# A two-layer encoder trunk on one core: order of work at the borders between its stages

## The chip, the core and the metric

The kernel runs on one core of a Trainium2 chip. A core has a matrix engine (TensorE, PE in the profile; its weight loads are shown apart as PEld), a vector engine (VectorE, DVE), an activation engine (ScalarE, ACT), a general engine (GpSimd, POOL) and a queue that issues nearly all transfers (SyncE, SP). Each engine runs its own list of instructions in order; where an instruction needs a result of another engine it waits, and all that stands behind it on its engine waits with it. The metric is the device time of one execution in microseconds (us); less is better.

## The reference

One token stream of 1024 rows and 1024 columns passes through a layer A and a layer B, all in fp32:

```python
h = rmsnorm(x, a_norm1); z = h @ a_w_in                  # layer A
tok   = gmlp_spatial_gating(gelu(z[u]), gelu(z[v]), ...)
mem_o = memory_attention(z[q], mem, ...)
x = x + concat(tok, mem_o) @ a_w_out
x = x + conv_ffn(rmsnorm(x, a_norm2), ...)
k, v, log_f_cum = split(rmsnorm(x, kv_norm) @ w_kv)      # shared by layer B
tok   = forgetting_attention(q, k, v, log_f_cum)         # layer B
x = x + concat(tok, mem_o) @ b_w_out
x = x + conv_ffn(rmsnorm(x, b_norm2), ...)
return rmsnorm(x, final_norm)

def conv_ffn(x, w_in, conv_w, conv_b, w_out):            # 1024 -> 2 x 2816 -> 1024
    h = x @ w_in
    hc = conv_b + sum(conv_w[j] * shifted(h, 2 - j) for j in range(3))
    gate, up = hc[:, :2816], hc[:, 2816:]
    return (silu(gate) * up) @ w_out
```

## The kernel before

Each fp32 matrix operand is split into a high part (a cast, on ACT) and a low part (value minus high part, on DVE or POOL), and each product is three matmuls: high by high, high by low, low by high. The feed-forward products are done block-wise with seven products in place of eight.

The stages, once for each layer:

- **Output projection** (`mix_out`, L575). For each of eight columns, in the order of the list `NORD` (0, 4, 1, 5, 2, 6, 3, 7), `mix_part` (L561) runs 48 matmuls (in layer B the first two columns have most of theirs behind them), and DVE adds the two halves from PSUM to the residual `xT[n]` (L573, the read-out). Then ACT scales (L583), the column is stored to `xdram`, its square goes into a sum `S` (L342 on POOL), and, every second column, `x_ops` (L598) forms the differences (`td`, L601) and splits (L346 on ACT, L347 on DVE) that the first stage of the feed-forward needs. The column's weights are a stream: raw tile `wr`, high part `wh` (L217, ACT), low part `wl` (L218, POOL).
- **Pairs** (`ffn`, function `pair`). 22 pairs of hidden blocks, seven products each. `w_prep` (L646 to L667) is a generator in seven steps that turns a pair's raw weights into seven split tiles `wo`: a cast on ACT (L646), a subtraction (L648; five of the seven on POOL, two on DVE), and four sums `ws` on DVE (L654, L655, L660, L667). In pair i it makes the weights of pair i+1; the weights of the first pair are made ahead of the pairs, by `drain(first[2])`, written ahead of `mix_out`. A pair's convolution (`conv`, L704 to L713) runs as another generator inside the next pair; that of the last pair was drained before the next stage is written.
- **Out phase** (`out_phase`). Seven products, each over six units (five of two blocks, one of one block): first `p1`, then `p5` and `p6` by turns, then `p3`, `p7`, `p2`, `p4`. The operands of a unit are loaded (`ro`, L793), some are combined on DVE (L813), and `both` splits them: a cast on ACT (L805) and a subtraction (L806) on DVE, or on POOL for one of the two operands where `both` is called with True. `ahead` keeps this two units ahead of PE. During `p1` the residual comes back from `xdram` in eight loads of 512 KB (L896); in layer B PE transposes it (L143, `to_rows`). `take` (L891) adds the finished PSUM banks to the residual. The last product, `p4`, ends column by column: its last two units run for one column, `take` reads it out, `on_done` handles it, then comes the next column. In layer B `on_done` is the final norm (L1640 on ACT, L1642, L1643 and L1647 on DVE, `rpow` L301 on POOL between them) and the store.
- At the end of layer A's out phase `before_last` is called after unit 2 of `p2` and after units 0 and 1 of `p4`: it loads the memory tokens, takes their norm, transposes them (`mem_t`: four steps of four PE transposes and a split of the result), and converts the first weight of the K/V projection.

A scheduler sets the order on each engine from the order in which the code is written, from readiness and from priorities; a `take` is fastened with `keep_in_program_order`. In layer A the residual arrives as high and low parts `xh`, `xl` and is put together again by `merge_residual`: eight additions of 128x1024 on POOL (L361), written before `mix_out`.

## Time and profile before

| | |
|---|---|
| median of 3 runs | 2295.09 us (2292.44 to 2295.14) |
| the profiled execution | 2295.76 us, of which the span in the trace is 2294.0 us |
| PE busy | 2150.1 us, 94% |
| DVE busy | 1724.6 us, 75% |
| ACT busy | 1035.8 us, 45% |
| POOL busy | 839.1 us, 37% |
| mean granted clock of PE | 0.982 of full speed |

The rows below come from the profile's page and from three kinds of answers of its trace. A row of the timeline gives the start and the length in us, the engine, the line, the operation, the tile written and the tiles read, the shape and how many such instructions follow each other; in brackets stands how long the engine was idle before it and what ended that wait. A row of the windows gives, for a stretch of the span, each engine's busy time with its count of instructions, then the granted clock of PE (1.00 is 2.4 GHz, 0.50 is 1.2 GHz), the share of time in which the DMA engines were busy, and GB/s.

### The profile page before, as it was taken

The numbers are of one execution on the slowest core, as the hardware profiler recorded it, in microseconds if no ns is written. First come the engines' busy times: TensorE is split into PE (matmuls) and PEld (weight loads), VectorE is DVE, ScalarE is ACT, GpSimd is POOL, SyncE is SP. The second block draws the span as 40 slices with busy tenths as digits, with TensorE's granted clock in tenths as the row PEclk, the third lists the DMA queues.
The fourth block names the chain that finished last, engine by engine and source line by source line (L and its number), as shares of the span: only waits on it lengthen the run. The fifth ranks groups of instructions, "written<-read, shape, count | busy, mean of one in ns | idle before, by whom it ended". The sixth has DMA issues, their size and how long they took to land.

```text
span 2294.0 us, 29435 instructions
## 1 busy us (share of the span) xinstructions
PE 2150.1 (94%) x10657; PEld 1791.2 (78%) x10657; DVE 1724.6 (75%) x2528; ACT 1035.8 (45%) x1732; POOL 839.1 (37%) x618
## 2 busy tenths in 40 slices
PE   7999799999999999989899999779999999999997
PEld 6998687777777878878688787667777777777886
DVE  4745748888888899566776777784888888886965
ACT  6562334343344434344555555653543344444433
POOL 1320633333333300351545554554333333331033
PEclk9999899999999999999999999999999999999999
DMA  5311221222222585513332333323222222256463
GB/s 177 93 29 37 65 97 61 83 83 83 77 80 83 192 279 178 180 33 85 109 78 80 91 98 98 86 73 101 67 83 83 75 82 83 68 201 236 147 202 111
DMA packets 219166, 243.55 MB, mean 106 GB/s; under 512 B 10074, under 2 KB 155648, under 8 KB 219020
## 3 DMA queue, kind: packets, MB, share of 16 engines
q1 hardware_dynamic: 218880, 241.63, 33.2%
q8 instruction: 84, 1.38, 0.3%
q14 instruction: 62, 0.51, 0.1%
q10 hardware_dynamic: 140, 0.04, 0.0%
HBM read 192.29 MB, written 38.85 MB: 101 GB/s over the span
## 4 chain that ended last, share of the span: by engine, by line
PE 30%; DVE 10%; issue 4%; ACT 3%; DMA 3%; POOL 2%; DVEq 0%; POOLq 0%; ACTq 0%; SPq 0%
PE pa L137 27%; PE pc L137 2%; DVE X L708 2%; DVE X L706 2%; PE pc L143 2%; DVE P L1368 1%; DMA nb<-cdram 1%; ACT P L1374 1%; POOL wo L648 1%; DVE X L347 1%; DVE ws L667 1%; DVE X L438 1%; DVE PTl L347 1%; DMA X<-xdram 1%; DVE U L727 1%
## 5 line engine op out<-in xcount | busy, mean ns | idle before, releaser
L137 PE MATMUL pa<-X,wo 128*128 128x512 f32 x3696 | 856.1, 392 | 25.5 <-DVE U L727 20.7
L137 PEld LDWEIGHTS pa<-X,wo 128*128 128x128 f32 x3696 | 690.9, 188 | 188.3 <-DVE U L727 37.7
L137 PE MATMUL pa<-X,X 128*128 128x512 f32 (+2 forms) x1868 | 445.3, 382 | 19.4 <-DVE sm L1368 8.5
L137 PEld LDWEIGHTS pa<-X,X 128*128 128x128 f32 x1868 | 343.9, 191 | 90.7 <-DVE sm L1368 8.7
L137 PE MATMUL pa<-X,wh 128*128 128x512 f32 (+1 forms) x1216 | 356.7, 403 | 17.8 <-ACT wh L217 8.6
L648 POOL TENSOR_TENSOR wo<-raw,wo 128x512 fp32r<-128x512 f32 x132 | 226.8, 1719 | 317.9 <-ACT wo L646 314.3
L137 PEld LDWEIGHTS pa<-X,wh 128*128 128x128 f32 x1216 | 220.9, 191 | 64.2 <-DVE X L347 11.2
L646 ACT CAST wo<-ws 128x512 fp32r<-128x512 f32 x176 | 109.1, 621 | 305.0 <-PE pa L137 293.1
L805 ACT CAST X<-ro 128x1024 fp32r<-128x1024 f32 (+1 forms) x142 | 130.5, 965 | 176.1 <-DVE ro L813 66.7
L137 PE MATMUL pa<-X,wl 128*128 128x512 f32 (+1 forms) x608 | 196.3, 402 | 12.4 <-POOL wl L218 12.3
L806 POOL TENSOR_TENSOR X<-ro,X 128x1024 fp32r<-128x1024 f32 (+1 forms) x34 | 89.1, 2630 | 320.2 <-ACT X L805 309.1
L648 POOL TENSOR_TENSOR wo<-ws,wo 128x512 fp32r<-128x512 f32 x88 | 116.4, 1323 | 219.6 <-ACT wo L646 212.9
L218 POOL TENSOR_TENSOR wl<-wr,wh 128x1024 fp32r<-128x1024 f32 (+1 forms) x41 | 102.2, 2494 | 213.4 <-ACT wh L217 208.1
L806 DVE TENSOR_TENSOR X<-ro,X 128x1024 fp32r<-128x1024 f32 (+1 forms) x108 | 137.0, 1294 | 49.8 <-ACT X L805 45.9
L137 PE MATMUL pa<-wh,X 128*128 128x256 f32 (+1 forms) x800 | 167.8, 288 | 0.0
L137 PEld LDWEIGHTS pa<-X,wl 128*128 128x128 f32 x608 | 111.2, 191 | 33.5 <-POOL wl L218 13.5
L137 PEld LDWEIGHTS pa<-wh,X 128*128 128x128 f32 x800 | 132.7, 190 | 1.6
L646 ACT CAST wo<-raw 128x512 fp32r<-128x512 f32 x132 | 81.1, 614 | 94.7 <-PE pa L137 89.9
L347 DVE TENSOR_TENSOR PTl<-pc,PTh 128x512 fp32r<-128x512 f32 (+1 forms) x152 | 90.8, 602 | 35.8 <-ACT PTh L346 34.6
L137 PE MATMUL pa<-wl,X 128*128 128x256 f32 (+1 forms) x400 | 113.8, 284 | 2.2 <-POOL wl L218 2.2
L467 POOL TENSOR_SCALAR P<-P,sm 128x128 f32<-128x128 f32 (+3 forms) x96 | 76.9, 802 | 90.2 <-DVE sm L1375 83.1
L1374 ACT ACTIVATE P<-P,sm 128x128 f32<-128x128 f32 (+3 forms) x96 | 74.7, 778 | 74.4 <-DVE sm L1368 72.4
(196 smaller groups left out, 3359.6 us busy)
## 6 DMA issues: line engine op xcount, KB each, us to landing
ro<-hdram SPq DMA_DIRECT2D x67, 512.0 KB
raw<-in_a_ffn_in_dram SPq DMA_DIRECT2D x44, 512.0 KB
hdram<-X SPq DMA_DIRECT2D x44, 512.0 KB
raw<-in_b_ffn_in_dram SPq DMA_DIRECT2D x44, 512.0 KB
ro<-in_a_ffn_out_dram SPq DMA_DIRECT2D x35, 512.0 KB
ro<-in_b_ffn_out_dram SPq DMA_DIRECT2D x32, 512.0 KB
X<-X SPq DMA_DIRECT2D x80, 128.0 KB
xdram<-X SPq DMA_DIRECT2D x16, 512.0 KB
```

The lines of the kernel that those rows point to most:

```text
L137: ins = nc.tensor.matmul(*a, **k)
L143: ins = nc.tensor.transpose(*a)
L218: eng.tensor_tensor(lo, raw, f32(hi), ALU.subtract)
L347: nc.vector.tensor_tensor(lo, src, f32(hi), ALU.subtract)
L467: nc.gpsimd.tensor_scalar(p, p, rinv, 1.0, ALU.mult, ALU.mult)
L646: nc.scalar.copy(h, src)
L648: eng.tensor_tensor(l, src, f32(h), ALU.subtract)
L706: nc.vector.scalar_tensor_tensor(t[:, 1:], h[:, :S - 1], w1, t[:, 1:], ALU.mult, ALU.add)
L708: nc.vector.scalar_tensor_tensor(t[:, 2:], h[:, :S - 2], w0, t[:, 2:], ALU.mult, ALU.add)
L805: nc.scalar.copy(h, src)
L806: (nc.gpsimd if pool else nc.vector).tensor_tensor(l, src, f32(h), ALU.subtract)
L1374: nc.scalar.activation(p[:, :n], p[:, :n], AF.Exp, bias=mn, scale=-1.0, accum_out=rs)
```

## The change

Five things are written in another place or for another engine:

1. `merge_residual` is gone. Layer A first converts the weights of the first two columns, then merges the residual in the order `NORD`, alternately on POOL and DVE (four each). The first pair's `w_prep` is no longer drained ahead of `mix_out`: `mix_out` calls `before(at)` ahead of each column, which takes one step (in layer A from the second column on, in layer B from the first); what is left is drained behind `mix_out`.
2. The convolution of the last pair is passed to `out_phase`, which takes two of its steps after each unit of `p1` and drains it before `take(a, 0, 0)`.
3. In `p1`, `both` is called without True, so that the six subtractions that stood on POOL in each layer go to DVE.
4. `before_last` is called after all four of the first units of `p4`; the memory transposes take one step at the second, third and fourth of these calls, and the fourth step behind the out phase.
5. The last read-outs, `take(a, 1, 0, [j])`, are not fastened to the program order.

```diff
-    def merge_residual(xh, xl):
-        res = []
-        for h, l in zip(xh, xl):
-            t = xt_()
-            nc.gpsimd.tensor_tensor(t, f32(l), f32(h), ALU.add)
...
-    def mix_out(tp, wget, kof, mh, ml, xT, g):
+    def mix_out(tp, wget, kof, mh, ml, xT, g, before):
...
         for at, n in enumerate(NORD):
+            before(at)
             xn = xT[n]
...
-                return both(a11s[u], lb(0, 0, u), True)
+                return both(a11s[u], lb(0, 0, u))
...
-        def take(bank, r, c, js=range(4)):
+        def take(bank, r, c, js=range(4), pin=True):
             for j in js:
                 d = acc[j + 4 * r][:, c * CH:(c + 1) * CH]
-                tc.keep_in_program_order(nc.vector.tensor_tensor(d, bank[j], d, ALU.add))
+                ins = nc.vector.tensor_tensor(d, bank[j], d, ALU.add)
+                if pin:
+                    tc.keep_in_program_order(ins)
...
-        def out_phase():
+        def out_phase(cg):
...
+                for _ in range(2):
+                    next(cg, None)
+            drain(cg)
             drain(rows)
             take(a, 0, 0)
...
             for u in range(NU - TAILU):
                 run(a, "p4", u, False)
-                if u < 2 and before_last is not None:
-                    before_last(u + 1)
+                before_last(u + 1)
...
-                take(a, 1, 0, [j])
+                take(a, 1, 0, [j], False)
                 on_done(j + 4, acc[j + 4])
...
-        drain(cg)
-        out_phase()
+        out_phase(cg)
...
-    xT = merge_residual(xh, xl)
...
     first = ffn_first(tp, a_ffn_in[0])
+    xT = {}
+
+    ast.conv(ast.at["o", NORD[0]] + 2)
+    for i, n in enumerate(NORD):
+        xT[n] = xt_()
+        (nc.vector if i % 2 else nc.gpsimd).tensor_tensor(xT[n], f32(xl[n]), f32(xh[n]), ALU.add)
+
+    def before_a(at):
+        if at > 0:
+            next(first[2], None)
+
+    ops, ssum_a = mix_out(
+        tp, lambda n: ast.use(("o", n), 1)[0], lambda at: KORD, mixh, mixl, xT, g_a2, before_a)
     drain(first[2])
-    ops, ssum_a = mix_out(tp, lambda n: ast.use(("o", n), 1)[0], lambda at: KORD, mixh, mixl, xT, g_a2)
...
         elif stage == 1:
             rm.append(mem_norm(tp, mtok, "T", 4))
             rm.append([])
-            drain(mem_t(mtok, rm[1]))
+            mt_g.append(mem_t(mtok, rm[1]))
         else:
-            wk_first[0] = wconv(wk_first[0], g_kv, True)
+            next(mt_g[0])
+            if stage == 2:
+                wk_first[0] = wconv(wk_first[0], g_kv, True)
...
     first = ffn_first(tp, b_ffn_in[0])
-    drain(first[2])
     ops, ssum = mix_out(
         tp, lambda n: wst.use(("o", n), 1)[0], lambda at: [6, 7] if at < NPRE else range(KT),
-        mixh, mixl, xT, g_b2)
+        mixh, mixl, xT, g_b2, lambda at: next(first[2], None))
+    drain(first[2])
```

How this moves instructions is shown at three places, before first, then after. Line numbers of the code behind the change are a few lower there (L648 reads L641, L793 reads L786, L217 and L218 stay).

POOL at the start of layer A's `mix_out`. `X` are the merged residual, `wo` the split weights of the first pair, `wl` the low parts of a column's weights, `S` the sum of squares. Before, these rows follow on six other merges and on the `wl` of the second column; the last row is the third column's:

```order
L361 TENSOR_TENSOR X_2418<-X_112,X_104 128x1024
L361 TENSOR_TENSOR X_2420<-X_113,X_105 128x1024
L648 TENSOR_TENSOR wo_2432<-raw_2426,wo_2432 128x512
L648 TENSOR_TENSOR wo_2440<-raw_2426,wo_2440 128x512
L648 TENSOR_TENSOR wo_2449<-ws_2430,wo_2449 128x512
L648 TENSOR_TENSOR wo_2452<-raw_2428,wo_2452 128x512
L648 TENSOR_TENSOR wo_2456<-ws_2444,wo_2456 128x512
L218 TENSOR_TENSOR wl_2616<-wr_2464,wh_2615 128x1024
```

Behind the change, from the `wl` of the second column on:

```order
L218 TENSOR_TENSOR wl_2419<-wr_2332,wh_2418 128x1024
L1206 TENSOR_TENSOR X_2422<-X_106,X_98 128x1024
L1206 TENSOR_TENSOR X_2426<-X_107,X_99 128x1024
L641 TENSOR_TENSOR wo_2502<-raw_2410,wo_2502 128x512
L1206 TENSOR_TENSOR X_2430<-X_108,X_100 128x1024
L1206 TENSOR_TENSOR X_2434<-X_109,X_101 128x1024
L218 TENSOR_TENSOR wl_2597<-wr_2439,wh_2596 128x1024
L218 TENSOR_TENSOR wl_2670<-wr_2505,wh_2669 128x1024
L342 TENSOR_TENSOR S_2438<-S_2438,sq_2562 128x1024
```

Between the second column's `wl` and the third's stand four merges and one subtraction instead of eight and five. On ACT one cast of the first pair, instead of seven, stands ahead of the third column's `wh`; on DVE four merges stand ahead of the first read-out, in place of four sums and two subtractions.

ACT in layer B's `mix_out`, between the third column and the fourth. `wo` are casts of the first pair's weights, `X<-td` and `X<-X` the casts of the differences of columns 0 and 4, `wh_14285` (before) and `wh_14275` (after) the fourth column's weights:

```order
L646 CAST wo_14127<-raw_14113 128x512
L646 CAST wo_14133<-ws_14130 128x512
L646 CAST wo_14136<-ws_14117 128x512
L646 CAST wo_14139<-raw_14115 128x512
L646 CAST wo_14143<-ws_14131 128x512
L346 CAST X_14196<-td_14194 128x512
L346 CAST X_14199<-X_14186 128x512
L346 CAST X_14204<-td_14202 128x512
L346 CAST X_14207<-td_14192 128x512
L346 CAST X_14212<-td_14210 128x512
L346 CAST X_14215<-X_14186 128x512
L217 CAST wh_14285<-wr_13977 128x1024
```

```order
L639 CAST wo_14199<-raw_14113 128x512
L346 CAST X_14177<-td_14175 128x512
L346 CAST X_14180<-X_14167 128x512
L346 CAST X_14185<-td_14183 128x512
L346 CAST X_14188<-td_14173 128x512
L217 CAST wh_14275<-wr_13977 128x1024
L346 CAST X_14193<-td_14191 128x512
L346 CAST X_14196<-X_14167 128x512
```

Four casts of the first pair and two of the differences moved behind the fourth column's `wh`. On DVE two sums (L660, L667) and one subtraction (L648) that stood ahead of these differences moved behind them, and on POOL two subtractions moved behind the fourth column's `wl`.

SP at the start of layer B's out phase, before and after. `X<-xdram` are the loads of the residual, `hdram<-X` the store of a pair's result, `ro` the operands:

```order
L793 DMA ro_18158<-in_b_ffn_out_dram 128x2x512
L793 DMA ro_18160<-in_b_ffn_out_dram 128x2x512
L793 DMA ro_18234<-in_b_ffn_out_dram 128x2x512
L793 DMA ro_18310<-in_b_ffn_out_dram 128x2x512
L793 DMA ro_18390<-in_b_ffn_out_dram 128x2x512
L896 DMA X_17950<-xdram 128x1024
L713 DMA hdram<-X_17904 128x1024
L896 DMA X_17952<-xdram 128x1024
```

```order
L786 DMA ro_18158<-in_b_ffn_out_dram 128x2x512
L891 DMA X_17939<-xdram 128x1024
L891 DMA X_17941<-xdram 128x1024
L891 DMA X_17943<-xdram 128x1024
L891 DMA X_17945<-xdram 128x1024
L891 DMA X_17947<-xdram 128x1024
L891 DMA X_17949<-xdram 128x1024
L891 DMA X_17951<-xdram 128x1024
L891 DMA X_17953<-xdram 128x1024
L786 DMA ro_18160<-in_b_ffn_out_dram 128x2x512
L786 DMA ro_18226<-hdram 128x2x512
L786 DMA ro_18234<-in_b_ffn_out_dram 128x2x512
```

The eight loads of the residual moved ahead of four loads of `p5`'s operands, and the store of the last pair's result moved behind them. POOL has nothing to do in `p1` any more, and PE's first transposes of the residual stand after the second unit of `p1`, where before they stood inside the third.

On DVE at the very end, where before each of the last four read-outs stood behind the whole final norm of the column before, the third read-out now stands right behind the second, and the fourth between the two small sums of the third column's norm.

## Rows read from the trace of the kernel before

**Rows 1.** The page: busy time of each engine, share of the span, instructions.
```profile
PE 2150.1 (94%) x10657; PEld 1791.2 (78%) x10657; DVE 1724.6 (75%) x2528; ACT 1035.8 (45%) x1732; POOL 839.1 (37%) x618
```

**Rows 2.** Timeline of PE at the start of layer A's output projection.
```profile
238.38 1.17 PE L137 MATMUL pa<-X,wh 128*128 128x512 f32 x4
...
261.43 1.20 PE L137 MATMUL pa<-X,wh 128*128 128x512 f32 x4 [0.58 <-ACT wh L217]
274.61 1.22 PE L137 MATMUL pa<-X,wl 128*128 128x512 f32 x2 [11.98 <-POOL wl L218]
275.63 1.91 PE L137 MATMUL pa<-X,wh 128*128 128x512 f32 x4
```

**Rows 3.** Timeline of the same stretch: POOL, then ACT, then DVE.
```profile
237.58 2.40 POOL L218 TENSOR_TENSOR wl<-wr,wh 128x1024 fp32r<-128x1024 f32 x1 [23.72 <-ACT wh L217]
243.53 21.24 POOL L361 TENSOR_TENSOR X<-X,X 128x1024 f32<-128x1024 f32 x8 [3.55 <-DVE X L347]
...
270.54 1.71 POOL L648 TENSOR_TENSOR wo<-ws,wo 128x512 fp32r<-128x512 f32 x1
272.21 5.14 POOL L218 TENSOR_TENSOR wl<-wr,wh 128x1024 fp32r<-128x1024 f32 x2
...
260.34 1.04 ACT L217 CAST wh<-wr 128x1024 fp32r<-128x1024 f32 x1
...
256.88 2.90 DVE L667 TENSOR_TENSOR ws<-raw,ws 128x512 f32<-128x512 f32 x1
```

**Rows 4.** Timeline at the start of layer A's out phase: PE, POOL, DVE.
```profile
808.06 8.23 PE L137 MATMUL pa<-X,X 128*128 128x512 f32 x35 [2.97 <-DVE X L806]
...
798.92 8.00 POOL L806 TENSOR_TENSOR X<-ro,X 128x1024 fp32r<-128x1024 f32 x3 [3.25 <-ACT X L805]
...
802.37 3.43 DVE L813 TENSOR_TENSOR ro<-ro,ro 128x1024 f32<-128x1024 f32 x1
```

**Rows 5.** Timeline of PE at the end of layer A's out phase.
```profile
983.29 0.66 PE L143 MATMUL pc<-ident,mt 128*128 128x128 f32 x4 [2.12 <-DVE X L347]
...
994.33 7.21 PE L137 MATMUL pa<-X,X 128*128 128x512 f32 x30 [0.84 <-DVE X L806]
1002.69 6.87 PE L137 MATMUL pa<-X,X 128*128 128x512 f32 x29 [1.15 <-DVE X L806]
```

**Rows 6.** Timeline in layer B's output projection: PE, DVE, POOL.
```profile
1549.70 2.50 PE L137 MATMUL pa<-X,wh 128*128 128x512 f32 x5 [7.54 <-ACT wh L217]
1552.56 1.22 PE L137 MATMUL pa<-X,wl 128*128 128x512 f32 x2 [0.36 <-POOL wl L218]
...
1534.57 0.68 DVE L655 TENSOR_TENSOR ws<-ws,raw 128x512 f32<-128x512 f32 x1
...
1534.67 2.86 POOL L342 TENSOR_TENSOR S<-S,sq 128x1024 f32<-128x1024 f32 x1 [1.17 <-ACT sq L338]
```

**Rows 7.** Timeline at the start of layer B's out phase: PE, POOL, SP.
```profile
2067.78 4.21 PE L137 MATMUL pa<-X,X 128*128 128x512 f32 x9 [4.05 <-POOL X L806]
...
2078.99 0.33 PE L143 MATMUL pc<-ident,X 128*128 128x128 f32 x1 [0.96 <-DMA X<-xdram]
...
2061.97 8.08 POOL L806 TENSOR_TENSOR X<-ro,X 128x1024 fp32r<-128x1024 f32 x2 [14.36 <-ACT X L805]
...
2053.29 8.13 SPq L793 DMA_DIRECT2D ro<-in_b_ffn_out_dram  x5
```

**Rows 8.** Windows of the same stretch, by 5 us.
```profile
2070.00:2075.00 5.00, 5.00 (x17) 3.85 (x16) 0.00 (x0) 0.00 (x0) 0.05 (x1) 0.70 1.03 415
```

**Rows 9.** Timeline of DVE at the end of layer B.
```profile
2275.09 0.69 DVE L891 TENSOR_TENSOR X<-pa,X 128x512 f32<-128x512 f32 x1 [8.87 <-PE pa L137]
...
2286.90 0.68 DVE L891 TENSOR_TENSOR X<-pa,X 128x512 f32<-128x512 f32 x1
2288.43 0.16 DVE L1642 TENSOR_TENSOR sm<-sm 128x1 f32<-128x1 f32 x1 [0.85 <-ACT jk L1640]
...
2289.50 1.41 DVE L1647 SCALAR_TENSOR_TENSOR X<-X,sm,X 128x512 f32<-128x512 f32 x2 [0.72 <-POOL sm L301]
```

More of the change, by code (lines that the diff above doesn't have):

```diff
@@ L679, in ffn_first, with ffn @@
         return in_srcs, w, w_prep(tp, raws, w, True)
-    def ffn(ops, ssum, first, w_out, cvs, on_done, tp, tm, before_last=None):
+    def ffn(ops, ssum, first, w_out, cvs, on_done, tp, tm, before_last=lambda stage: None):
         in_srcs, w, _ = first
@@ L951, in out_phase @@
                 run(c, "p2", u, True)
-                if u == 2 and before_last is not None:
+                if u == 2:
                     before_last(0)
@@ L1232 @@
     GSEQ = [2, 0, 1]
-    wk_first = []
+    wk_first, mt_g = [], []
     def before_last(stage):
```

3 lines of the change are left out of this document (1 added, 2 removed).

## The prediction, made before the changed kernel was run

> **What bounds the kernel now.** I read the page first: PE is busy for 94% of the span and no other engine for more than 75% [rows 1]. The arithmetic of PE is the same before and after, so the change can only win idle time of PE and time in which its clock is low. That is why I went through PE's timeline for idle stretches, and then for each through the timelines of the engine named in its bracket, to see what stood ahead of the awaited instruction. The stretches that the change touches are few. The largest is the third column of layer A's output projection: PE waits 0.58 us for the column's high part and then 11.98 us for its low part [rows 2]; the low part is the 272.21 row of POOL, which stands behind 21.24 us of merges and five subtractions [rows 3]. Next come layer B's projection (7.54 and 0.36 us, [rows 6]), the start of its out phase (4.05 us for POOL and three waits for loads of the residual, the last 0.96 us, some 2.2 us together [rows 7]), layer A's out phase at its start (2.97 us, [rows 4]) and its end (2.12, 0.84 and 1.15 us, [rows 5]). The end of the kernel is different: there DVE works alone, in a chain of four read-outs and norms [rows 9].
>
> All sums are made against the profiled execution, 2295.76 us, which is 0.67 us above the median of the runs shown; the last step takes that off.
>
> **Layer A's projection: -14 us.** Two columns take 22.5 us at full clock (238.38 to 261.43 less the wait [rows 2]), so PE comes to the third at 260.85 and to its first low part about 1 us later. Behind the change POOL goes through four merges and one subtraction there, from 243.53 on. A merge beside DVE's work took 21.24/8 = 2.65 us, a subtraction 1.71 [rows 3]: the end is 243.53 + 4 x 2.65 + 1.71 = 255.8, and the low part, 5.14/2 = 2.57 us, is done at 258.4, some 3 us early. Its high part no longer stands behind seven casts that wait for slow sums on DVE (such as the 2.90 us of the 256.88 row), but behind one, and is ready near 250. The four merges that went to DVE run beside POOL's at about one for one, so the first read-out comes near 257 instead of 265, and the fourth column's low part near 264, needed at 272. The 12.56 us of idle go in full. The clock gives more: behind the wait two matmuls took 1.22 us and four 1.91, where four take 1.17 at full clock [rows 2], so about 1.5 us. That makes 14.1, and I take 14. If the third column still waits for a merge or two, 9 us are left; more than 14.5 cannot be had here.
>
> At this place a rule can be weighed. The rows show that POOL's 128x1024 operation takes 2.40 us with DVE quiet and 2.65 us in the row of merges, while DVE's 512-wide sum beside it takes 2.90 in place of 0.68 [rows 3, 6]: the two go at about one operation each per 2.65 us. The Trainium skill (SBUF — State Buffer, "Who interferes with whom") says that a DVE instruction with two SBUF inputs and a GpSimd instruction that reads SBUF exclude each other, and that the second to issue is blocked until the first ends. By that rule the split of the merges would save little: an estimate by it is 4 x (2.40 + 1.2) = 14.4 us in place of 10.6, the low part at 262.2, and a wait of about half a microsecond; the sum would be 1 us smaller.
>
> **Layer B's projection: -5.5 us.** Before, the fourth column's high part stood on ACT behind six casts of differences that DVE made late, since two sums and a subtraction of the first pair, and POOL's addition into `S`, lay ahead of them. Hand trace from the rows: the sum at 1534.57 ends at 1535.25; the first difference runs beside POOL's `S` (1534.67, 2.86 us) and ends near 1538, the second beside one subtraction of POOL (1.71) near 1539.8; a subtraction and the third difference at 0.68 each end at 1541.2; two casts of about 0.6 us and the high part (1.04 [rows 3]) end near 1543.4 and the low part near 1546. PE is there at 1549.70 - 7.54 = 1542.16 [rows 6]: it waits 1.3 us and, after five matmuls, some 1.6 us more. 7.9 - 2.9 = 5.0 us; and five matmuls that took 2.50 us at low clock [rows 6] show another 1 us lost, half of which I count back. Bounds: 3 (if the differences still go at POOL's pace) to 8.
>
> **Layer B's out phase: -6 us.** The 4.05 us were for a subtraction on POOL that ran beside DVE's work at 8.08/2 = 4.04 us each [rows 7]. It goes to DVE, which does a 128x1024 at about 1.2 us (half of a 2.5 us pair, and a third of the slowed 3.43 [rows 4]) and had nothing to do for most of this stretch. The loads of the residual now stand before four operand loads. Before, five operand loads took 8.13 us to issue from 2053.29 on, since they waited for free tiles [rows 7], and the eight residual loads came behind. Now they can start at about 2054, as soon as the queue has room; eight of 512 KB at the 415 GB/s of that stretch [rows 8] take 10.1 us, so with what lies in the queue ahead they end near 2069. PE comes to the first transposes at 2067.78 - 4.05 = 2063.7 and to the last tile's, one unit later, near 2070: about even. I count the 4.05, the 2.2 less 1.5 for waits that remain, and for the clock 1.3 (nine matmuls took 4.21 us instead of about 2.2 [rows 7], and a part of that stays with the waits that remain). DVE then waits for the first operand load behind the residual, due near 2072; the fifth unit's subtraction behind it is needed near 2079, so some 2 us are left over. Bounds: -9, if no wait remains, to +2.
>
> **Layer A's out phase, start: -3 us.** The same move without transposes. PE's 2.97 us came from DVE operations of 3.43 us beside POOL's three (8.00 us) [rows 4]; with POOL idle, DVE gains more than 6 us over these operations, and carries three more of 1.2 us by then. Here all operand loads of `p1` stand ahead of the residual. Next late would be `p5`'s loads, some 5 us early by the same rate. Bounds: -3.5 to +2.
>
> **Layer A's out phase, end: -3 us.** Eight transposes of memory tokens came at once, and PE waited 2.12 us for the splits that free their banks [rows 5]. With one step of four transposes to each unit of `p4`, the split has a unit's time, and this wait goes; the clock behind it (a dip, not a stop) is worth up to 1.5. The 0.84 and 1.15 us are for subtractions on DVE; POOL keeps its part in `p4`, so I count half of them. Against that, one split of 0.68 us [rows 6] now falls behind the out phase, into the chain of small operations before the K/V projection: 0.7 to 1.3 us. 2.1 + 1.0 + 1.0 - 1.1 = 3. Bounds: -5 to +1.
>
> **The first pairs: +1.3 us.** The steps of `w_prep` are spread to the last column of each projection, so that a sum (0.68) and a subtraction on POOL (1.71) [rows 3, 6] fall next to the last column's read-out. In each layer this is 0 to 1.7 us; 0.65 each.
>
> **The end: -2.5 us.** A column's chain takes (2286.90 - 2275.09)/3 = 3.94 us: read-out to sum 1.53 us, sum to the end of the scalings 2290.91 - 2288.43 = 2.48 us [rows 9]. PE has delivered the later columns long before. With the second and third read-outs made together, the 1.53 us of the third and fourth column run beside the norm of the column before. The second column's sum stays where it was, the third's scalings end near 2285.9 and the fourth's near 2288.4, in place of 2290.91. Two gaps of about 1.25 us each. Nothing hides this stretch, and nothing can take it back but the last store, which follows the scalings as before. Bounds: -2.2 to -2.8.
>
> **Sum.** -14 - 5.5 - 6 - 3 - 3 + 1.3 - 2.5 = -32.7 us; 2295.76 - 32.7 = 2263.1, less 0.67 is 2262.4. I say 2263 us.
>
> **Rivals.** (a) Layer A's third column still waits: a tile or bank that a merge needs is free later than 243.53, so that the low part comes 8 us later. 2263 + 8 - 3 (its margin) + 3 (clock and the next column) = 2271 us. For it: the merges now write tiles in another order; against it: before, they started right behind DVE's last split [rows 3]. (b) Loads bound the out phases. If the residual loads start only at about 2061, as before, PE's transposes, now earlier in its list, stand about 10 us instead of 6.2 at low clock, DVE stands at the operand load behind them, and layer A loses its gain: 6 + 4 + 3 + 3 = 16 us more, 2279 us. For it: 415 GB/s with the engines fully busy [rows 8] is all that this stretch ever moved; against it: before, issue was held up by the five operand loads, of which four now come later. (c) Slower: the first pair's weights arrive behind their products. Each of the 14 needs a cast, at times a sum, and a subtraction on POOL, 0.6 + 0.7 + 1.7 = 3 us. If every product waited for its own step, the two layers would pay 42 us, and the time would be 2305 us; it turns slower than before from 33/14 = 2.4 us per product on. Against it: six of seven steps stand ahead of the last column's read-out in the new order, and a product takes longer than a step. (d) Most gains come back as other waits: 2285 us.
>
> **Chances.** Forecast 0.74, (a) 0.08, (b) 0.12, (c) 0.02, (d) 0.04. The range reaches from 2254 (the better bounds of two of the large terms) to 2279, which takes in (a) and (b) and leaves (d) and (c) out. A change within 0.2% (4.6 us) can't be told from none: 2290.5 to 2299.7. Faster 0.95, the same 0.03, slower 0.02.
>
> **What would show each step.** No wait for `wl` in the first four columns of layer A, and PE at its clock from 238 to 327. A wait of 1 to 4 us for the fourth column in layer B. No POOL work in `p1`, and waits for `xdram` of under 2 us in layer B. The last four read-outs 0.6 us apart for the second and third. I am wrong in the main if layer A's projection takes over 95 us (ideal 8 x 11.2 = 90), or if PE stands for over 6 us at the first transposes of layer B's out phase.

## The result, and the profile after

The changed kernel takes 2259.81 us (median of 4 runs, 2258.52 to 2262.19) against 2295.11 us (2292.44 to 2297.73) for the kernel before in the same comparison: a ratio of 0.9847, 95% interval 0.983 to 0.9864, or 35.3 us less. The forecast was 2263 us with a range from 2254 to 2279. The total is right to 3 us and six of its eight terms to 1.3 us, but the two terms for the starts of the out phases rest on the wrong cause, and one term (layer A's out end) can't be put down to the change, as the experiments show.

The page of the changed kernel, to be held against [rows 1]:

```profile
PE 2140.5 (95%) x10657; PEld 1785.8 (79%) x10657; DVE 1719.6 (76%) x2544; ACT 1036.4 (46%) x1732; POOL 794.0 (35%) x602
```

PE has the same 10657 instructions in 36 us less time (profiled span 2257.7 us against 2294.0). POOL has lost 45 us of work and 16 instructions; DVE has 16 more and still no more busy time.

To see where the time went, I cut PE's timeline at fixed places in its list of instructions; each stage then holds the same instructions in all these kernels, some of them in another order. Layer A's output projection, for example, runs from its first product with `wh` to the first with `wo`, 238.38 to 342.04 us before and 236.86 to 326.07 after; layer B's begins one transpose earlier. "First pair" is the first 127 (layer A) or 133 (layer B) matmuls behind a projection, "out start" the first 172 (layer A) or 231 (layer B) instructions of PE in an out phase, "A out end" the 270 ahead of the sixteenth product of the K/V projection. The end is counted from PE's last matmul to the last scaling.

| stage, us | before | after | difference | forecast |
|---|---|---|---|---|
| A projection | 103.66 | 89.21 | -14.5 | -14 |
| A first pair | 30.21 | 32.77 | +2.6 | +0.65 |
| A out start | 42.51 | 38.99 | -3.5 | -3 |
| A out end | 66.08 | 64.32 | -1.8 | -3 |
| B projection | 98.22 | 93.36 | -4.9 | -5.5 |
| B first pair | 30.19 | 30.17 | 0.0 | +0.65 |
| B out start | 56.96 | 45.78 | -11.2 | -6 |
| the end | 9.74 | 7.14 | -2.6 | -2.5 |

These sum to -35.8 us. The rest of the span's 36.3 is not in the code that changed: up to layer A's projection 1.5 us less, attention 1.0 more.

**Layer A's projection.** Timelines of POOL, then DVE, then ACT in the changed kernel (start us, us, engine, line, operation, output<-inputs, shapes, count, and in brackets the idle time before and who ended it); the rows before are [rows 3]:

```profile
242.03 5.94 POOL L1206 TENSOR_TENSOR X<-X,X 128x1024 f32<-128x1024 f32 x2 [3.56 <-DVE X L347]
247.93 1.30 POOL L641 TENSOR_TENSOR wo<-raw,wo 128x512 fp32r<-128x512 f32 x1
249.18 6.72 POOL L1206 TENSOR_TENSOR X<-X,X 128x1024 f32<-128x1024 f32 x2
255.86 3.40 POOL L218 TENSOR_TENSOR wl<-wr,wh 128x1024 fp32r<-128x1024 f32 x1
```

```profile
244.47 1.23 DVE L1206 TENSOR_TENSOR X<-X,X 128x1024 f32<-128x1024 f32 x1 [2.52 <-POOL X L1206]
248.00 8.98 DVE L1206 TENSOR_TENSOR X<-X,X 128x1024 f32<-128x1024 f32 x3 [2.31 <-POOL X L1206]
256.90 1.27 DVE L565 TENSOR_TENSOR X<-pa,X 128x512 f32<-128x512 f32 x2
```

```profile
247.76 1.05 ACT L217 CAST wh<-wr 128x1024 fp32r<-128x1024 f32 x1 [1.81 <-PE pa L137]
```

The third column's low part is done at 255.86 + 3.40 = 259.26, where before it ended near 275, and PE doesn't wait for it. But PE comes to the column at 236.86 + 22.5 = 259.4 and needs the low part 1 us later: the margin is about 1 us, not 3. A row with `x2` or `x3` gives a sum, and its parts differ: the first merge on POOL ran alone and took 2.41 us, the other three, each beside a merge on DVE, 3.46, 3.39 and 3.38.

**Layer B's projection.** PE in the changed kernel, against the 7.54 and 0.36 us of [rows 6]:

```profile
1525.38 1.20 PE L137 MATMUL pa<-X,wh 128*128 128x512 f32 x4 [0.99 <-ACT wh L217]
1529.09 1.22 PE L137 MATMUL pa<-X,wl 128*128 128x512 f32 x2 [2.51 <-POOL wl L218]
```

**Layer B's out phase.** PE, then SP, against [rows 7]; PE has no bracket from the first product to the last transpose:

```profile
2029.89 11.05 PE L137 MATMUL pa<-X,X 128*128 128x512 f32 x48
2040.78 0.49 PE L143 MATMUL pc<-ident,X 128*128 128x128 f32 x3
```

```profile
2030.12 0.37 SPq L786 DMA_DIRECT2D ro<-in_b_ffn_out_dram  x1
2030.54 5.91 SPq L891 DMA_DIRECT2D X<-xdram  x8
```

**The end.** DVE, against [rows 9]: the third and second read-outs stand together (`x2`), and the fourth lies between two small operations.

```profile
2241.34 0.69 DVE L884 TENSOR_TENSOR X<-pa,X 128x512 f32<-128x512 f32 x1 [8.59 <-PE pa L137]
...
2245.28 1.28 DVE L884 TENSOR_TENSOR X<-pa,X 128x512 f32<-128x512 f32 x2
...
2249.28 0.69 DVE L884 TENSOR_TENSOR X<-pa,X 128x512 f32<-128x512 f32 x1
...
2253.14 1.42 DVE L1657 SCALAR_TENSOR_TENSOR X<-X,sm,X 128x512 f32<-128x512 f32 x2 [0.72 <-POOL sm L301]
```

From the first read-out to the last scaling it is 13.22 us, before 15.82.

### The profile page after: what moved, and what is told of

It is laid out like the page before. It is cut to its first block, busy times and chain, and to the rows that moved or that the text cites. A ratio compares the mean times of both kernels' runs of the same rounds, so it can differ in the third digit from the quotient of the medians.

```text
span 2257.7 us, 29405 instructions
## 1 busy us (share of the span) xinstructions
PE 2140.5 (95%) x10657; PEld 1785.8 (79%) x10657; DVE 1719.6 (76%) x2544; ACT 1036.4 (46%) x1732; POOL 794.0 (35%) x602
## 4 chain that ended last, share of the span: by engine, by line
PE 66%; DVE 18%; issue 6%; ACT 5%; POOL 3%; DMA 3%; ACTq 0%; DVEq 0%; POOLq 0%; SPq 0%
PE pa L137 59%; PE pc L137 5%; DVE X L701 4%; DVE X L699 4%; PE pc L143 2%; DVE ws L660 1%; DVE P L1378 1%; DMA nb<-cdram 1%; DVE U L720 1%; DVE X L347 1%; POOL wo L641 1%; DVE X L430 1%; ACT P L1384 1%; POOL wl L218 1%; DVE PTl L347 1%
## 5 line engine op out<-in xcount | busy, mean ns | idle before, releaser
L137 PE MATMUL pa<-X,X 128*128 128x512 f32 (+2 forms) x1868 | 440.1, 379 | 14.3 <-DVE sm L1378 9.1
L641 POOL TENSOR_TENSOR wo<-raw,wo 128x512 fp32r<-128x512 f32 x132 | 223.8, 1695 | 319.2 <-ACT wo L639 315.6
L641 POOL TENSOR_TENSOR wo<-ws,wo 128x512 fp32r<-128x512 f32 x88 | 116.3, 1321 | 233.5 <-ACT wo L639 226.9
L799 POOL TENSOR_TENSOR X<-ro,X 128x1024 fp32r<-128x1024 f32 (+1 forms) x24 | 59.5, 2482 | 344.8 <-ACT X L798 336.2
L218 POOL TENSOR_TENSOR wl<-wr,wh 128x1024 fp32r<-128x1024 f32 (+1 forms) x41 | 104.0, 2538 | 183.6 <-ACT wh L217 178.6
L799 DVE TENSOR_TENSOR X<-ro,X 128x1024 fp32r<-128x1024 f32 (+1 forms) x118 | 142.6, 1237 | 31.6 <-ACT X L798 29.2
```

What stands on the lines that cost most here:

```text
L137: ins = nc.tensor.matmul(*a, **k)
L218: eng.tensor_tensor(lo, raw, f32(hi), ALU.subtract)
L641: eng.tensor_tensor(l, src, f32(h), ALU.subtract)
L799: (nc.gpsimd if pool else nc.vector).tensor_tensor(l, src, f32(h), ALU.subtract)
```

## The experiments

All start from the changed kernel, and each undoes or moves one part. All medians, with their ratios to the kernel before in the same comparison, and the stages (us) of the profiled execution:

| kernel | median | ratio (95%) | A proj. | A first pair | A out start | A out end | B proj. | B first pair | B out start |
|---|---|---|---|---|---|---|---|---|---|
| after | 2259.81 | 0.9847 (0.983-0.9864) | 89.21 | 32.77 | 38.99 | 64.32 | 93.36 | 30.17 | 45.78 |
| u1a | 2272.12 | 0.9906 (0.9891-0.9922) | 105.14 | 28.83 | 38.99 | 66.18 | 93.53 | 30.19 | 45.77 |
| u1c | 2253.84 | 0.9816 (0.9795-0.9838) | 89.16 | 28.82 | 38.99 | 64.32 | 93.45 | 30.23 | 45.75 |
| m8d | 2255.39 | 0.9829 (0.9815-0.9844) | 89.21 | 32.41 | 38.99 | 64.30 | 90.80 | 30.17 | 45.69 |
| u1b | 2263.95 | 0.9862 (0.9845-0.988) | 89.21 | 32.31 | 38.99 | 64.33 | 98.21 | 30.17 | 46.95 |
| u2 | 2271.62 | 0.990 (0.9884-0.9916) | 89.21 | 32.35 | 41.91 | 64.32 | 93.56 | 31.56 | 57.87 |
| u3 | 2258.75 | 0.985 (0.9834-0.9866) | 89.21 | 32.83 | 39.37 | 64.33 | 93.62 | 30.20 | 46.87 |
| u6 | 2267.40 | 0.9886 (0.9867-0.9904) | 89.21 | 32.36 | 39.36 | 64.30 | 90.79 | 30.17 | 53.82 |
| u7 | 2260.3 | 0.9855 (0.9838-0.9872) | 89.21 | 32.37 | 38.99 | 64.30 | 90.81 | 30.19 | 47.59 |
| u4 | 2257.05 | 0.9834 (0.9817-0.9852) | 89.21 | 32.43 | 38.99 | 66.05 | 93.53 | 30.20 | 45.85 |
| u5 | 2261.47 | 0.9858 (0.9841-0.9876) | 89.21 | 32.37 | 38.99 | 64.30 | 93.54 | 31.55 | 45.75 |
| v1 | 2252.87 | 0.9816 (0.9799-0.9833) | 89.21 | 28.83 | 38.99 | 64.33 | 87.98 | 33.99 | 45.71 |
| v2 | 2251.76 | 0.9812 (0.9797-0.9826) | 89.21 | 30.19 | 38.99 | 65.90 | 87.92 | 30.20 | 45.76 |

What the same code does from one execution to the next must be known to read this: the attention stage between them took 492.25 to 497.93 us in these thirteen executions, the projection of layer B 90.8 or 93.4 us with one and the same code around it, its first pair 30.2 or 31.55. In the three executions at 90.8 PE waits 1.3 us for the fourth column's low part, in the others at 93.4 to 93.6 it waits 2.5 us, and the granted clock falls behind that. Layer A's out end takes 64.3 us or about 66 with the same code (u1a and v2), and layer A's first pair 28.83 (v1) or 30.19 (v2). So stages that repeat to 0.1 us carry the verdicts, and neither a stage that takes two values nor a difference of medians under some 4 us does.

**u1a: layer A's projection starts as before.** All eight merges on POOL, and the first pair ahead of the projection:

```diff
+    xT = {}
+    for n in range(KT):
+        xT[n] = xt_()
+        nc.gpsimd.tensor_tensor(xT[n], f32(xl[n]), f32(xh[n]), ALU.add)
...
-    ast.conv(ast.at["o", NORD[0]] + 2)
-    for i, n in enumerate(NORD):
-        xT[n] = xt_()
-        (nc.vector if i % 2 else nc.gpsimd).tensor_tensor(xT[n], f32(xl[n]), f32(xh[n]), ALU.add)
+    drain(first[2])
...
     def before_a(at):
-        if at > 0:
-            next(first[2], None)
+        pass
```

> The changed kernel with the start of layer A's projection as before: eight merges on POOL, the first pair's weights made ahead of the projection. Theory (POOL's queue ahead of the third column's low part): the wait of about 12 us comes back and the first pair wins back 2.6 us that it lost, so 12 us slower than the changed kernel, 2272 us. Rival (the gain of layer A came from the clock or from the start of the run): under 5 us slower.

The whole is 12.3 us slower. The projection is back at 105.14 us, 15.9 us longer, while the first pair is 3.9 us shorter than in the changed kernel. POOL's timeline is that of [rows 3] again (`243.51 21.24` for the eight merges). The two parts of this edit had to be told apart.

**u1c: the merges as changed, the first pair's weights at once.**

```diff
+    drain(first[2])
...
     def before_a(at):
-        if at > 0:
-            next(first[2], None)
+        pass
```

> The changed kernel, but with layer A's first pair made ahead of the projection; the merges stay split between POOL and DVE. It tells the two halves of the change at this place apart. If the merges alone were the block: the projection stays at 89.2 us and the first pair falls to about 29 us, 2256 us. If the first pair's steps count as well: POOL has 14 us of merges and a subtraction, then the third column's low part, so that PE does not wait there, but four subtractions of 1.7 us each stand ahead of the fourth column's low part, and DVE's sums ahead of the first read-outs: 0 to 4 us of wait in the projection, 2257 to 2260 us.

The projection keeps its whole gain (89.16 us) and the first pair takes 28.82 us. So in layer A all of the gain comes from the merges, whose place, order and engines changed together (which of these counts is not told apart, except by m8d below); spreading the pair's weights by steps only costs there, 32.77 - 28.82 = 3.9 us. The changed kernel's wait, in PE's timeline and its windows (from:to, us, busy time of PE, PEld, DVE, ACT, POOL, then the granted clock as a share of 2.4 GHz, DMA share and GB/s):

```profile
335.41 1.43 PE L137 MATMUL pa<-X,wo 128*128 128x512 f32 x5 [1.43 <-ACT X L346]
```

```profile
335.00:340.00 5.00, 4.59 (x23) 4.24 (x24) 4.45 (x7) 1.93 (x4) 0.00 (x0) 0.76 0.00 0
340.00:345.00 5.00, 5.00 (x14) 3.87 (x13) 2.64 (x6) 2.57 (x5) 0.00 (x0) 0.55 0.00 0
```

The casts it waits for read the last column's differences, which DVE made late. Each pair makes its sums in the order L647, L648, L653, L660, so the sum at 328.51 is the first pair's last, ahead of the last read-outs, and the sum at 331.70 is already the second pair's: it took 1.80 us in place of 0.68, beside the second pair's first subtraction on POOL. DVE, then POOL:

```profile
328.51 0.68 DVE L660 TENSOR_TENSOR ws<-raw,ws 128x512 f32<-128x512 f32 x1
...
331.70 1.80 DVE L653 TENSOR_TENSOR ws<-raw,raw 128x512 f32<-128x512 f32 x1
```

```profile
331.32 1.64 POOL L641 TENSOR_TENSOR wo<-raw,wo 128x512 fp32r<-128x512 f32 x1
```

In u1c the second pair's sum has its usual length, as POOL's subtraction starts behind it, at 334.47:

```profile
332.27 0.68 DVE L653 TENSOR_TENSOR ws<-raw,raw 128x512 f32<-128x512 f32 x1
```

The first pair's sum (0.68) and the longer sum of the second (1.12) make up the 1.8 us by which the awaited cast comes later than in u1c, counted from the pair's first product. In u1c this wait is absent and the granted clock is 1.00 from 330 to 350 us.

**m8d: all eight merges on DVE.**

```diff
-        (nc.vector if i % 2 else nc.gpsimd).tensor_tensor(xT[n], f32(xl[n]), f32(xh[n]), ALU.add)
+        nc.vector.tensor_tensor(xT[n], f32(xl[n]), f32(xh[n]), ALU.add)
```

> The changed kernel with all eight merges on DVE, POOL free for the low parts. It measures what the split of the merges is worth. If the two engines exclude each other (a pair of merges taking about 1.2 + 2.4 us), the eight take 9.8 us on DVE, less than the 13.8 us that POOL and DVE took together, and the third column's low part is ready several us earlier; the time does not change, 2259.8 us, since PE did not wait there any more. If they overlapped freely, the split version would have been the faster one to read the columns out.

DVE, then POOL:

```profile
241.86 12.61 DVE L1206 TENSOR_TENSOR X<-X,X 128x1024 f32<-128x1024 f32 x8
```

```profile
246.08 1.70 POOL L641 TENSOR_TENSOR wo<-raw,wo 128x512 fp32r<-128x512 f32 x1 [7.73 <-ACT wo L639]
248.78 3.47 POOL L218 TENSOR_TENSOR wl<-wr,wh 128x1024 fp32r<-128x1024 f32 x1 [1.01 <-ACT wh L217]
```

DVE alone does the eight in 12.61 us, with two operations of POOL beside it (9.8 expected: six took 1.22 us each, two beside POOL 2.32 and 3.42); two engines took from 242.03 to 256.98, with one operation of POOL between. The low part is done at 252.25, 7 us earlier, and PE's stage is the same 89.21 us, as it doesn't wait either way. The median is 4.4 us lower, but the stages show 2.6 of that in layer B's projection, which this edit doesn't touch: no gain can be claimed, only that POOL's help is worth nothing here, and that the gain doesn't need two engines.

**u1b: layer B's first pair at once.**

```diff
     first = ffn_first(tp, b_ffn_in[0])
+    drain(first[2])
...
-        mixh, mixl, xT, g_b2, lambda at: next(first[2], None))
-    drain(first[2])
+        mixh, mixl, xT, g_b2, lambda at: None)
```

> The changed kernel with layer B's first pair made ahead of its projection again. Theory: the fourth column waits 7 to 8 us again, the projection takes 98.2 us in place of 93.4: 5 us slower, 2264.7 us. Rival (the projection's gain belongs to something else, such as the state in which the attention ends): under 2 us slower.

The projection goes back to 98.21 us, the before's 98.22, with the before's wait in PE's timeline ([rows 6]: 7.54):

```profile
1530.38 2.50 PE L137 MATMUL pa<-X,wh 128*128 128x512 f32 x5 [7.53 <-ACT wh L217]
```

In layer B, then, the steps are the whole gain of the projection, and cost nothing in the pair. The two layers differ: the same edit gains in one and loses in the other.

**u2: the last convolution ahead of the first product, as before.** POOL stays out of `p1`.

```diff
+        drain(cg)
         out_phase(cg)
```

> The changed kernel with the last pair's convolution drained ahead of the out phase again; POOL stays out of p1. Theory (POOL's slow subtractions were the wait, the loads of the residual only a part): in layer B the waits for residual loads come back in part, 2 to 5 us slower, 2263 us; layer A unchanged within 1 us. Rival (the place of the residual loads in SP's queue is what counts): 8 to 11 us slower, PE standing at the transposes.

**u3: POOL's part in `p1`, as before.** The convolution stays inside the product.

```diff
-                return both(a11s[u], lb(0, 0, u))
+                return both(a11s[u], lb(0, 0, u), True)
```

> The changed kernel with one of the two subtractions of p1 on POOL again. Theory (POOL beside DVE is the wait): 8 to 12 us slower over both layers, 2269 us, with waits of PE for POOL or DVE in p1 of 3 us or more in each layer. Rival (load order): under 3 us slower.

These two tell the two halves of the change at the out phases apart, and the theory of both expectations lost. With the convolution ahead, all of layer B's gain is lost (57.87 us, before 56.96) and most of layer A's (41.91; 42.51), though POOL does nothing in `p1`. With POOL back, 46.87 and 39.37. Of its 1.1 us in layer B nothing is sure to be POOL's: u1b, where POOL isn't in `p1`, has 46.95 there; nor of the 0.4 us in layer A (u6: 39.36). Under u2, DVE, then ACT, then PE:

```profile
2034.49 2.47 DVE L699 SCALAR_TENSOR_TENSOR X<-h,cvb,X 128x1023 f32<-128x1023 f32 x2
2036.88 2.47 DVE L701 SCALAR_TENSOR_TENSOR X<-h,cvb,X 128x1022 f32<-128x1022 f32 x2
2039.27 1.22 DVE L799 TENSOR_TENSOR X<-ro,X 128x1024 fp32r<-128x1024 f32 x1
```

```profile
2038.25 1.06 ACT L703 ACTIVATE X<-X 128x1024 f32<-128x1024 f32 x1 [3.20 <-DVE X L701]
2039.21 2.93 ACT L798 CAST X<-ro 128x1024 fp32r<-128x1024 f32 x3
```

```profile
2042.81 2.36 PE L137 MATMUL pa<-X,X 128*128 128x512 f32 x9 [1.31 <-DVE X L799]
2047.19 0.33 PE L143 MATMUL pc<-ident,X 128*128 128x128 f32 x1 [2.02 <-DMA X<-xdram]
```

ACT's `Silu` waits 3.20 us for DVE's convolution, and three casts of operands stand behind it; DVE's subtractions of the operands (L799) begin at 2039.27, behind the convolution. In the changed kernel two of them come first, and `Silu` only at 2050.68, 12.4 us later:

```profile
2029.78 1.21 DVE L799 TENSOR_TENSOR X<-ro,X 128x1024 fp32r<-128x1024 f32 x1
...
2031.51 1.21 DVE L799 TENSOR_TENSOR X<-ro,X 128x1024 fp32r<-128x1024 f32 x1
...
2034.70 1.28 DVE L699 SCALAR_TENSOR_TENSOR X<-h,cvb,X 128x1023 f32<-128x1023 f32 x1
```

SP stood at five operand loads for 9.55 us (in the changed kernel one load stands there, 0.37 us), with the residual behind them; of SP's waits at these loads 3.5 us are for DVE's convolution (L701), 2.6 for a load of an operand, 1.3 for an operand sum on DVE (L806) and 0.5 for PE:

```profile
2030.24 9.55 SPq L786 DMA_DIRECT2D ro<-in_b_ffn_out_dram  x5
2039.83 0.46 SPq L891 DMA_DIRECT2D X<-xdram  x1
```

PE's five waits for `xdram` are 2.02, 0.96, 0.95, 0.81 and 0.80 us, 5.5 together where before it was 2.2. Its wait for the operand's subtraction is 1.31 us, where it waited 4.05 for POOL [rows 7]: DVE did take 2.7 us off that wait, the loads took as much back, and the stage is no shorter.

**u6: the convolution ahead, the residual's loads written ahead of the whole out phase.** As the late loads are what PE waits for in u2, is their place in SP's queue enough?

```diff
+        drain(cg)
         out_phase(cg)
...
+            load_xT()
             for u in range(NU):
                 run(a, "p1", u, True)
                 if u == 0:
-                    load_xT()
```

> The last pair's convolution drained ahead of the out phase as before, but the eight loads of the residual written ahead of p1's first unit, so that SP has four of them right behind the first of the five operand loads, and the other four behind the store of the convolution's result. Theory (SP's queue was the block: the residual loads stood behind operand loads that wait for tiles which the late convolution holds): the start of layer B's out phase takes 46 to 50 us in place of 57.9, 2262 us. Rival (the convolution's own time on DVE and ACT ahead of p1's splits is the block): it stays at 56 to 58 us, 2271 us.

It gives back 4 of the 12 us (53.82, in neither range). Four of the eight loads go at 2025.68; then SP stands at the store of the convolution's result, and the other four come behind it. All of PE's waits in this stage (3.38, 0.86 and 0.81 us) are for these loads, and the first comes right behind four transposes of tiles that are there:

```profile
2025.68 2.67 SPq L891 DMA_DIRECT2D X<-xdram  x4
2034.64 0.32 SPq L706 DMA_DIRECT2D hdram<-X  x1
2035.01 2.26 SPq L891 DMA_DIRECT2D X<-xdram  x4
```

```profile
2039.89 0.45 PE L143 MATMUL pc<-ident,X 128*128 128x128 f32 x1 [3.38 <-DMA X<-xdram]
```

**u7: the opposite, the convolution late, four operand loads ahead of the residual's.**

```diff
                 if u == 0:
+                    ahead(4 + AHEAD)
                     load_xT()
```

> Where layer B's out phase gained 11 us. As the changed kernel, the last convolution still inside the first product, but four loads of p5's operands are written ahead of the eight loads of the residual (as they stood before the change). Load order theory: SP stands at these operand loads until tiles come free, the residual comes some 8 to 10 us later, PE waits several times for xdram at its transposes, the start of layer B's out phase takes 52 to 58 us instead of 45.8 and the whole 2266 to 2272 us. Rival (the late convolution itself leaves DVE and ACT free for the operands, and the place of the loads matters little): that start takes 46 to 48 us and the whole 2258 to 2262 us. In layer A, where the residual isn't transposed here, neither expects a change (39.0 us).

My theory by then, that the order of the loads makes the difference, lost: 47.59 us, in the rival's range. SP still stands at the operand loads (6.0 us in three waits, for DVE's subtractions L799), and the first load of the residual goes 8.5 us behind the phase's first product, in u2 9.8. But all eight then follow within 4.9 us; in u2, where the store of the convolution's result stands among them, the eighth goes 7.3 us behind the first. PE waits once:

```profile
2025.26 3.56 SPq L786 DMA_DIRECT2D ro<-in_b_ffn_out_dram  x3
2030.81 2.64 SPq L786 DMA_DIRECT2D ro<-hdram  x2
2033.49 4.93 SPq L891 DMA_DIRECT2D X<-xdram  x8
```

```profile
2039.94 0.33 PE L143 MATMUL pc<-ident,X 128*128 128x128 f32 x1 [1.38 <-DMA X<-xdram]
```

With u2 and u6 this fills a table of four for the start of layer B's out phase: convolution late, 45.8 (residual's loads early) and 47.6 us (behind operand loads); convolution ahead, 53.8 and 57.9. The place of the convolution is worth 8 to 10 us, that of the loads as written 2 to 4. This isn't a clean division: with the convolution ahead the loads were never all early, as the store of its result stands in SP's queue in front of four loads (u6) or seven (u2). How much of the 8 to 10 us comes by this store, and how much by the convolution's own time on DVE and ACT, no run here tells.

**u4: the memory tokens' transposes at once.**

```diff
             mt_g.append(mem_t(mtok, rm[1]))
+            drain(mt_g[0])
...
-            next(mt_g[0])
+            next(mt_g[0], None)
```

> The changed kernel with the sixteen memory transposes made at once again; the calls at all units of p4 stay. Theory (PE waited for the splits between the two halves of the transposes): the stretch from the fifth unit of p2 to the K/V projection takes 66.1 us as before, in place of 64.3, so 2 us slower, 2261.6 us. Rival (that stretch gained because the last read-outs are not fastened): no change in this stretch.

The wait is back, 2.10 us in place of [rows 5]'s 2.12, and the stage takes 66.05 us (before 66.08):

```profile
965.77 0.91 PE L143 MATMUL pc<-ident,mt 128*128 128x128 f32 x4 [2.10 <-DVE X L347]
```

That the 1.8 us come of this edit is not shown, though. u1a and v2 have the transposes spread as in the changed kernel and the same four waits as there (3.8 and 3.5 us in all), and took 66.18 and 65.90 us; what they have more is a stretch of low clock, which in v2 stands here (0.66; the changed kernel has 1.00 in all of this stage):

```profile
980.00:985.00 5.00, 4.31 (x11) 3.18 (x12) 3.12 (x5) 2.00 (x2) 1.54 (x2) 0.66 0.32 105
```

u4 has such a stretch behind its wait, also 0.66. The waits themselves add up to 4.0 us in u4 and 3.5 in the changed kernel. The rival, that the unfastened read-outs gave the gain, is out: u5 fastens them and has 64.30 us. The median shows nothing either way (2257.05); attention took 493.46 us in this execution and 497.93 in the changed kernel's.

**u5: the last read-outs pinned.**

```diff
-                take(a, 1, 0, [j], False)
+                take(a, 1, 0, [j])
```

> The changed kernel with the last read-outs fastened to program order again. Theory: the chain on DVE at the end takes 3.94 us a column again, 2.5 us longer from the end of PE to the end of the scalings, 2262.3 us. Rival (the store behind it ends at the same time anyway): no change.

The chain from the first read-out to the last scaling is 15.82 us again, as before, and 13.22 in the changed kernel. In the median that is 1.7 us, within the spread, and the stage alone carries the verdict.

**v1 and v2: the steps of the first pair elsewhere.** After u1b and u1c the steps should stand early in layer A's projection, and in layer B behind the fourth column, with none by the last. In v1:

```diff
     def before_a(at):
-        if at > 0:
-            next(first[2], None)
+        for _ in range((0, 1, 1, 1, 2, 2, 0, 0)[at]):
+            next(first[2], None)
...
+    def before_b(at):
+        for _ in range((0, 0, 0, 0, 3, 2, 2, 0)[at]):
+            next(first[2], None)
...
-        mixh, mixl, xT, g_b2, lambda at: next(first[2], None))
+        mixh, mixl, xT, g_b2, before_b)
```

> A version that may beat both: in layer A the first pair's steps end one column earlier (two at the fifth and the sixth column), in layer B they begin at the fifth column (3, 2, 2). Theory (the wait of the fourth column in layer B and the slower first pair in layer A are both due to steps that fall next to the differences): layer B's projection 93.4 to 89.5 us, layer A's first pair 32.7 to 29.5: 2253 us. Rival (POOL has too little time in the later columns: per column a low part 2.4, a square 2.8 and two or three subtractions of 1.7 us in 11.1): new waits for low parts, 2260 us or more.

v2 has (0, 0, 0, 0, 4, 3, 0, 0) in layer B.

> As the version before, but layer B's first pair takes its seven steps at the fifth and sixth column (4, 3). Theory (the last steps fell so late that the first pair's splits ran into the second pair's sums): layer B's projection stays at 88.0 us, its first pair falls from 34.0 to 30.2: 2249 us. Rival (four steps at one column make a low part late): the projection is 2 us or more longer, 2253 us.

v1's layer B projection takes 87.98 us with no wait for the fourth column, but its first pair 33.99: the same late sum and a wait of 1.39 us for ACT's casts, and a low clock behind it, as in layer A of the changed kernel. In v2 the pair is at 30.20, and v2 has the lowest median, 2251.76 us (2250.2 to 2251.97; ratio 0.9812), 8.1 us below the changed kernel; from v1 and u1c the medians alone don't tell it apart. Its stages give 5.4 us in layer B's projection and 2.6 in layer A's first pair, less the 1.6 us by which layer A's out end is longer in this execution.

## Why the prediction came out as it did

**Layer A's projection: right, and for its reason**, with one size off. POOL's queue ahead of the low part was the cause (u1a, u1c). But a pair of merges, one on each engine, took 3.38 to 3.46 us, where I had taken 2.65 from a row whose first three merges ran alone (2.40 each) and whose others ran beside DVE's shorter operations (2.79 to 2.86). The 3 us of margin were about 1. The rule of the Trainium skill that I set beside it (SBUF — State Buffer, "Who interferes with whom") gave an estimate of 2.40 + 1.2 = 3.6 us a pair; the rows lie between the two and nearer to the rule, and m8d agrees with what it implies, that two engines on such operations do no more than DVE alone. The wait that it would have led to didn't come, by that 1 us.

**Layer A's first pair: the step that failed is the price of 0.65 us.** I priced one sum and one subtraction of the first pair, 0 to 1.7 us. The chain through the last column's differences lengthened by 1.8 us, of which only 0.68 is the first pair's sum; the rest came by the second pair's sum, which fell beside POOL. Behind the wait of 1.43 us the clock fell to 0.76 and 0.55 for ten us. 2.6 us against before, 3.9 against u1c; the two differ by the clock, which read 0.77 and 0.89 there in the kernel before and 1.00 in u1c, behind equal stops. In layer B the steps are not spread to the last column, though I wrote so: they begin at the first column, and the last of the seven stands ahead of the seventh (its sum at 1550.46, where the first pair begins at 1585.39), so that it costs nothing.

**Layer B's projection: right.** The two waits were worked out by hand as 1.3 and 1.6 us, and are 0.99 and 2.51. What I hadn't looked for is that the steps could begin later: v2 takes another 5.4 us.

**The out phases: the sum of the two terms was too small (9 us, measured 14.7), and the attribution was wrong.** The step that failed is the path: I credited the 4.05 us of layer B and the 2.97 of layer A to POOL's subtraction going to DVE, as if the stage were shorter by a wait that ends. The row of POOL in [rows 7] says in its own bracket that it started at ACT's cast, which came behind the convolution on ACT and DVE, as under u2. Its 8.08 us are also not twice 4.04:

```profile
2061.97 5.76 POOL L806 TENSOR_TENSOR X<-ro,X 128x1024 fp32r<-128x1024 f32 x1 [14.36 <-ACT X L805]
2067.69 2.36 POOL L806 TENSOR_TENSOR X<-ro,X 128x1024 fp32r<-128x1024 f32 x1
```

The first, for which PE waited, ran beside three operations of DVE. So POOL was slow there, and with DVE in its place the wait is 1.31 us (u2); but with the convolution ahead the loads of the residual come next and hold the stage as long, and the whole gain is lost. u3 puts POOL back behind the late convolution and loses at most 1.1 us. The size failed at two places: I left 1.5 us for waits on the residual, and none remained (in u1b and u3 one, of 0.67 and 1.05); and I counted 1.3 us for the clock. Of the 11.2 us the waits were 4.05 + 2.2, which leaves about 5 us, in which PE stood for nothing but ran at a low clock: it was granted 0.70 at [rows 8], and is granted 1.00 in the changed kernel:

```profile
2040.00:2050.00 10.00, 9.99 (x56) 7.91 (x55) 1.22 (x1) 2.60 (x5) 0.00 (x0) 1.00 1.01 388
```

Rival (b), the residual's loads late, didn't come; SP issued them at 2030.54, 0.65 us behind the phase's first product, as forecast (1.5 us), and the four operand loads behind them do not hold the phase.

**Layer A's out phase, end: -1.8 instead of -3, and not shown to come of the change.** The wait of 2.12 us went, as u4 confirms, but the claim that half of the others would go too was wrong: four waits stand there now, for DVE and POOL. PE in the changed kernel:

```profile
967.30 5.29 PE L137 MATMUL pa<-X,X 128*128 128x512 f32 x22 [1.31 <-POOL X L799]
...
973.70 5.52 PE L137 MATMUL pa<-X,X 128*128 128x512 f32 x23 [0.44 <-DVE X L799]
...
982.55 0.50 PE L137 MATMUL pa<-X,X 128*128 128x512 f32 x1 [1.13 <-DVE X L799]
983.68 6.65 PE L137 MATMUL pa<-X,X 128*128 128x512 f32 x28 [0.62 <-POOL X L799]
```

Together 3.5 us, where 4.1 stood: the idle time moved, and most of the 1.8 us is the clock, which u1a and v2 lost again with the same waits.

**The end: right** (-2.5, measured -2.6), since DVE's chain stands alone there and can be summed from its rows.

That the total was right is in part luck, by errors of both signs: the out phases gave 5.7 us more than forecast, layer A's pair and out end 3.1 less. Left open: why the fourth column's low part in layer B is late by 1.3 us in some executions and by 2.5 in others with the same code, why attention spreads by 5.7 us, when the clock falls behind a short stop, and what DVE, ACT and the store in SP's queue are each worth in the convolution's delay, which no run here told apart.

## What to carry to other kernels

Where an engine is named as the one that PE waits for, read that engine's own bracket, and what PE would wait for next, before pricing its work: in u2 a faster engine took 2.7 us off one wait, and the next took them back, since what stood ahead of both had stayed. Work that has no reader nearby (here a convolution, whose result goes out to memory) belongs behind the preparation of the next product on every queue that both use, its store in the queue of the loads included: here that was worth 8 to 10 us. When preparatory steps are spread over a stage, put them where their engines wait anyway and away from its last read-out, and judge each place by itself: the same spreading gained 4.9 us in layer B and lost 3.9 us in layer A.

## What the runs showed of the hardware

- Two engines on 128x1024 additions from SBUF were not faster than one. Alone a merge took 1.22 us on DVE and 2.41 on POOL; side by side each took 3.38 to 3.46, nearly the sum. DVE alone did all eight in 12.61 us, two operations of POOL beside it (one of them 3.47 us in place of 2.40); the two engines took 14.95, with one.
- Either engine can be the one that is slowed. In the kernel before, POOL's subtraction took 5.76 us beside three operations of DVE that kept their 1.22 us each, and the next, with DVE idle, 2.36. In u3 it took 2.73, and the step of the convolution that DVE began beside it 3.40 in place of 1.28.
- Short stops of PE cost more than their length. In layer B's out phase waits of 6.2 us went with a loss of about 11, and the single stop of 1.43 us in layer A's first pair with windows at 0.76 and 0.55 of the clock; in u1c, with stops of 0.55 and 0.49 us at the same place, the clock stayed at 1.00. But it isn't told by the stops alone: in the kernel before, stops of 0.56 and 0.49 us at that place went with windows at 0.77 and 0.89, and the four waits at the end of layer A's out phase left the clock at 1.00 in the changed kernel and went with 0.66 in v2.
